# Query projection of an attention layer by Strassen pairs, its gate in two passes, and whole tiles stored at a time

## The chip, the cores and the metric

The kernel runs on one core of a Trainium2 chip. The metric is the device time of one execution in microseconds (us). Engines are named as in the profile: PE is TensorE's matmul, PEld its weight load, DVE VectorE, ACT ScalarE, POOL GpSimd, SP the SyncE queue that only issues DMAs.

## The reference

A two-layer decoder trunk on 1024 tokens of width 1024, in float32: a recurrent layer, an FFN, then one set of keys and values, an attention layer with three branches (compressed, selected, window), a second FFN and a norm. The change touches the queries and gates of the attention layer, and how heads are stored:

```
u = h @ w_q
q = (u[..., :N_HEADS * D_QK] * (D_QK ** -0.5)).reshape(B, S, G, HPG, D_QK)
gates = jax.nn.sigmoid(u[..., N_HEADS * D_QK:] + gate_bias).reshape(B, S, G, HPG, N_BRANCH)
q_rope = apply_partial_rope(q)
```

Here h is the normed residual (1024 tokens x 1024), w_q has 16 heads x 96 + 48 columns, and the 16 heads form 4 groups of 4. The plain q meets the compressed keys, q_rope the selected and window keys.

## The kernel before

**Layout and precision.** Activations lie transposed, features on partitions and tokens along the free dimension: 8 blocks of 128 features x 1024 tokens. A float32 product is made of three matmuls on values split in a high and a low part (`split`, L231 to L234: ACT copies the high part, DVE subtracts it): high x high, high x low, low x high (`mm3`). A projection of one tile of 128 outputs over 512 tokens (`proj`) is thus 8 blocks x 3 = 24 matmuls into one PSUM bank, 48 for all tokens. The norm's row scale is applied to the result (`rb1`, a 128x1024 tile that holds the scale of each token), its feature gain to the operand (`xg`).

**Query tiles.** A group's 4 heads x 96 features are packed in three tiles of 128: two with 64 unrotated features of two heads each (j = 0, 1), one with the 32 others of all four heads (j = 2), of which 24 are rotated (`rope`: a shuffle and three DVE operations of 128x1024). Four groups make 12 tiles.

**Stages.** `run` calls `rglru` (with the first FFN), `kv`, `qphase`, then the rest of the attention and `wo` (with the second FFN). `kv` makes values, the key tiles (`heads`, with `store_split` and `store_heads`), the raw compressed keys and values, and the two compression products (`cmp_hidden`, names ph), between which the query's operands are made: eight loads h1l of the residual from `h1d`, each split by `xg` into xh and xl. `qphase` computes the gate (names pg, gt; its weight has 48 columns, `wn=48`), the rest of the compression (`cmp_out`), then the query tiles group by group (`qheads`, names pn, n). A group is written to three DRAM tensors (`qd`: high part, low part, unrotated), by `store_heads` in eight SP DMAs each, per head. The attention (`attention`) is a generator: its first steps load masks, queries and keys and are taken between the groups, and group 3 is handed to it as filler, of which it takes one half-tile every `FE` = 4 turns of its loop. `load_q` fetches the queries of one of the 32 steps (4 groups x 8 blocks of 128 tokens).

**Strassen form.** The two FFNs are computed with seven products in place of eight (names pa, pb, pc, so, L745): the 8 blocks of features and the 1024 tokens are each halved, so the operand has four parts, and from them come B11, T1, T2, T3, B21, T4, B22. Each product is 4 blocks x 3 = 12 matmuls of 512 tokens, and each weight operand is split by `sop` (128x512) a few products ahead. There two tiles of outputs, gate and value, are a pair.

**Order and buffers.** All large tiles come from one pool of 49 buffers of 128x1024 (`slot`), all PSUM tiles from 8 banks (`ps`). A buffer's next writer waits until its last reader is done, a store's landing included. The order on each engine is fixed when the program is built: a planner takes instructions in program order, those under `high_priority` (weight loads and splits) earlier. `wget` returns the next weight, loads `ld` and splits `sp` ahead.

Of the kernel before, what the change touches and what calls it, by code (L numbers as in the profile page):

```python
# [27 lines left out]
QPRE = 5  # L28
# [12 lines left out]
FIL = 5  # L41
QLT = 1
FI0 = 1
FE = 4
XA = 3
# [26 lines left out]
Q_LAST = Q_ORDER  # L72


class Trunk:
# [44 lines left out]
    def weights(self):  # L120
# [18 lines left out]
        for b in range(2):  # L139
            for j in range(3):  # L140
                w.append((f"k{b}_{j}", d["w_k"][b, j], 1024))
# [4 lines left out]
        for j in range(6):  # L146
            w.append((f"w1k{j}", d["w1_k"][j], 1024))
        for j in range(4):
            w.append((f"w1v{j}", d["w1_v"][j], 1024))
        w.append(("gate", d["w_gate"], 384))  # L150
        w.append(("w2", d["w2"], 320, 0))
        for g in range(4):
            for j in (2, 0, 1):
                w.append((f"q{g}_{j}", d["w_q"][g, j], 1024))
# [30 lines left out]
    def pair_load(self, src, n):  # L185
        def f(t):
            self.nc.sync.dma_start(t.rearrange("p (b c) -> p b c", b=2)[:, :, 0:n],
                                   src[:, :, 0:n].rearrange("b p c -> p b c"))
        return f
# [446 lines left out]
    def sop(self, src):  # L636
        t = self.slot("so", F32R)
        self.split(t[:, 0:512], t[:, 512:1024], src)
        return t
# [698 lines left out]
    def heads(self, keys, xs, rb):  # L1338
        nc = self.nc
        n = []  # L1340
        for key in keys:
            w = self.wget(key)
            t = self.slot("n")
            for c0 in (0, 512):
                p = self.ps("pn")
                self.proj(p, w, xs, c0)
                nc.vector.tensor_tensor(t[:, c0:c0 + 512], p, rb[:, c0:c0 + 512], ALU.mult)
            n.append(t)
        return n
# [10 lines left out]
    def store_heads(self, dst, n):  # L1360
        nc = self.nc
        for h in range(4):
            a = (h % 2) * 64
            nc.sync.dma_start(dst[h, 0:64], n[h // 2][a:a + 64, :])
            nc.sync.dma_start(dst[h, 64:96], n[2][32 * h:32 * h + 32, :])

    def store_split(self, dhi, dlo, n):
        his, los = [], []
        for t in n:
            hi, lo = self.slot("nh", F32R), self.slot("nl", F32R)  # L1370
            self.split(hi, lo, t)
            his.append(hi.bitcast(F32))
            los.append(lo.bitcast(F32))
        self.store_heads(dhi, his)
        self.store_heads(dlo, los)
# [19 lines left out]
    def kv(self, kvp):  # L1395
# [6 lines left out]
        self.kd = self.dram("kd", [2, 2, 4, 96, S])  # L1402
# [36 lines left out]
        for b in range(2):  # L1439
            n = self.heads([f"k{b}_{j}" for j in range(3)], xs, rb)  # L1440
            n[2] = self.rope(n[2])
            self.store_split(self.kd[b, 0], self.kd[b, 1], n)
# [41 lines left out]
        hk = self.cmp_hidden("w1k", imk)  # L1484
        del imk
        self.xq = []

        def xq(k0, k1):
            for k in range(k0, k1):
                h = self.slot("h1l")  # L1490
                nc.gpsimd.dma_start(h, self.h1d[k])
                self.xq.append(self.xg(h, 2, k))

        xq(0, XA)
        hv = self.cmp_hidden("w1v", imv)
        xq(XA, KD)
        return hv, hk

    def cmp_out(self, hv, hk):
        nc = self.nc  # L1500
        w2 = self.wget("w2")
# [37 lines left out]
    def cmp_hidden(self, key, im):  # L1539
# [4 lines left out]
        for q in range(len(im)):  # L1544
            w = self.wget(f"{key}{q}")
            for j in range(4):
                for a, b in ((0, 0), (0, 1), (1, 0)):
# [5 lines left out]
                    i += 1  # L1553
        bias = self.small("hb", 2)
# [6 lines left out]

    def qphase(self, hid):
        nc, d = self.nc, self.d
        xs, self.xq = self.xq, None
        rb = self.rb1
        w = self.wget("gate")
        gt = self.slot("gt")
        for c0 in (0, 512):
            p = self.ps("pg")
            self.proj(p[0:48, :], w, xs, c0, wn=48)  # L1570
            nc.vector.tensor_tensor(gt[0:48, c0:c0 + 512], p[0:48, :], rb[0:48, c0:c0 + 512], ALU.mult)
        nc.scalar.activation(gt[0:48, :], gt[0:48, :], AF.Sigmoid, bias=self.cv[0:48, C_GB:C_GB + 1])
        self.cmp_out(*hid)
        self.qd = [self.dram(f"qd{j}", [4, 4, 96, S]) for j in range(3)]
        def qheads(g):
            nonlocal rb
            n = []
            for j in (2, 0, 1):
                w = self.wget(f"q{g}_{j}")
                t = self.slot("n")  # L1580
                for c0 in (0, 512):
                    p = self.ps("pn")
                    self.proj(p, w, xs, c0)
                    nc.vector.scalar_tensor_tensor(t[:, c0:c0 + 512], p, QSCALE, rb[:, c0:c0 + 512],
                                                   op0=ALU.mult, op1=ALU.mult)
                    if j == 1 and c0:
                        if g == 3:
                            xs.clear()
                    else:
                        yield  # L1590
                n.append(t)
                if j == 2:
                    r2 = self.rope(t)
            n = n[1:] + n[:1]
            if g == 3:
                self.cos = self.sin = self.rb1 = None
                rb = t = w = None
# [674 lines left out]
```

## Time and profile before

| | us |
|---|---|
| median of 3 runs | 2631.3 (2630.43 to 2632.89) |
| the profiled execution | 2628.91 |
| its span on the chip | 2627.1 |
| 1234 to 1265: compression products, ph | 31 |
| 1265 to 1376: gate, rest of the compression, query tiles up to the first half of group 3 | 111 |
| 1376 to 1428: the attention begins, the other five halves as filler | 52 |
| 1428 to 1890: the attention without filler | 462 |

The span is divided by the profile's own time, which begins with the first instruction of the program. Busy times of engines overlap, since they run beside each other; what counts in a stretch is which engine has no gap. Matmuls are pipelined: the duration of one is longer than the distance to the next.

### The profile page before, as it was taken

The page shows a single profiled execution, that of the slowest core. Times are in us where ns is not written, and L with a number is a line of the kernel's source. Part 1 is how long each engine was busy: PE and PEld are TensorE (multiplying, and loading weights), DVE is VectorE, ACT ScalarE, POOL GpSimd, SP SyncE. Part 2 cuts the span into 40 slices and gives each one's busy share as a digit, 9 for nine tenths or more (in the row PEclk, how much of TensorE's full clock was granted, in tenths as well). Part 3 has the DMA queues.
Part 4 walks back from the last instruction along what each step waited for, and adds up shares of the span by engine and source line. Part 5 has one row for each costly group of instructions (what it writes and reads, how often), then busy time and mean ns, then how long its engine had stood idle before and what let it go on. Part 6 is the DMA issues. An engine that isn't in the chain of part 4 may idle for free.

```text
span 2627.1 us, 36460 instructions
## 1 busy us (share of the span) xinstructions
PE 2595.6 (99%) x12490; PEld 2165.5 (82%) x12490; DVE 1856.2 (71%) x3683; ACT 1310.4 (50%) x2573; POOL 934.4 (36%) x1101
## 2 busy tenths in 40 slices
PE   8999999999999999999999999999999999999998
PEld 7887888888888888888888888888887888888886
DVE  7686778655555887537447989988879555557976
ACT  4556656432323544414316888888865223324534
POOL 0111242443434330201004766666543343434333
PEclk9999999999999999999999999999999999999999
DMA  4233796666566993544384412221695666558971
GB/s 161 90 125 114 291 230 179 151 152 152 150 145 179 252 243 80 181 124 156 131 245 128 118 62 70 67 68 47 149 253 138 145 158 163 151 134 224 245 185 64
DMA packets 189160, 400.59 MB, mean 152 GB/s; under 512 B 18592, under 2 KB 68128, under 8 KB 188976
## 3 DMA queue, kind: packets, MB, share of 16 engines
q1 hardware_dynamic: 119280, 245.24, 28.6%
q0 software_dynamic: 68320, 151.09, 27.3%
q8 instruction: 99, 1.62, 0.2%
q10 hardware_dynamic: 1376, 1.94, 0.2%
q14 instruction: 85, 0.70, 0.1%
HBM read 308.55 MB, written 83.36 MB: 149 GB/s over the span
## 4 chain that ended last, share of the span: by engine, by line
PE 80%; DVE 5%; DMA 2%; issue 2%; ACT 0%; POOL 0%; SPq 0%; POOLq 0%; DVEq 0%; ACTq 0%
PE pb L745 13%; PE pa L745 8%; PE pc L745 8%; PE pU L1097 8%; PE pn L241 8%; PE psc L241 6%; PE pV L1097 5%; PE pt L1914 4%; PE pU L1283 3%; PE pW L1097 2%; PE po L1945 2%; PE po L1946 2%; PE py L241 2%; PE pV L1283 2%; PE pkc L241 1%
## 5 line engine op out<-in xcount | busy, mean ns | idle before, releaser
L233 ACT ACTIVATE so<-wr 128x512 fp32r<-128x512 f32 (+1 forms) x504 | 296.2, 612 | 188.6 <-DMA wr<-w_dn 79.2
L234 DVE TENSOR_TENSOR so<-wr,so 128x512 fp32r<-128x512 f32 (+1 forms) x504 | 343.3, 710 | 64.6 <-ACT so L233 63.9
L745 PE MATMUL pb<-so,so 128*128 128x512 f32 x1584 | 381.4, 391 | 4.2 <-DVE so L234 1.8
L745 PEld LDWEIGHTS pb<-so,so 128*128 128x128 f32 x1584 | 298.0, 188 | 67.7 <-DVE so L234 2.3
L745 PE MATMUL pc<-so,so 128*128 128x512 f32 x1056 | 256.2, 389 | 0.0
L745 PE MATMUL pa<-so,so 128*128 128x512 f32 x1056 | 250.9, 389 | 0.0
L1097 PE MATMUL pU<-so,so 128*128 128x512 f32 x1056 | 244.2, 389 | 0.0
L192 POOL DMA_DIRECT2D wr<-w_gu x176 | 162.3, 1068 | 224.3 <-DVE so L234 182.6
L745 PEld LDWEIGHTS pa<-so,so 128*128 128x128 f32 x1056 | 198.3, 188 | 41.1
L745 PEld LDWEIGHTS pc<-so,so 128*128 128x128 f32 x1056 | 198.3, 188 | 41.1
L1097 PEld LDWEIGHTS pU<-so,so 128*128 128x128 f32 x1056 | 198.1, 188 | 41.1
L241 PE MATMUL psc<-kl,ql 96*128 96x512 f32 (+2 forms) x960 | 230.2, 365 | 0.8 <-DVE cst L1738 0.5
L773 ACT ACTIVATE ev<-ev 128x512 f32<-128x512 f32 x44 | 27.8, 632 | 328.8 <-POOL ev L772 328.8
L234 DVE TENSOR_TENSOR thl<-pt,thl 128x512 fp32r<-128x512 f32 x264 | 176.7, 683 | 13.4 <-ACT thl L233 12.2
L241 PEld LDWEIGHTS psc<-kl,ql 96*128 96x128 f32 x960 | 163.8, 189 | 22.1 <-issue 1.1
L233 ACT ACTIVATE thl<-pt 128x512 fp32r<-128x512 f32 x264 | 150.1, 594 | 44.2 <-PE pt L1914 38.0
L234 DVE TENSOR_TENSOR wl<-wr,wh 128x1024 fp32r<-128x1024 f32 (+3 forms) x95 | 104.9, 1112 | 66.8 <-ACT wh L233 55.8
L192 POOL DMA_DIRECT2D wr<-w_dn x96 | 91.0, 1192 | 148.3 <-DVE so L234 62.1
L772 POOL TENSOR_TENSOR ev<-ev,rb 128x512 f32<-128x512 f32 x44 | 59.8, 1359 | 220.1 <-DVE ev L771 220.1
L233 ACT ACTIVATE wh<-wr 128x1024 fp32r<-128x1024 f32 (+3 forms) x95 | 89.6, 964 | 66.4 <-DMA wr<-w_q 19.9
L1097 PE MATMUL pV<-so,so 128*128 128x512 f32 x528 | 121.6, 389 | 0.0
L1097 PEld LDWEIGHTS pV<-so,so 128*128 128x128 f32 x528 | 99.1, 188 | 20.6
(390 smaller groups left out, 5929.2 us busy)
## 6 DMA issues: line engine op xcount, KB each, us to landing
wr<-w_gu SPq DMA_DIRECT2D x110, 512.0 KB, 4.8
wr<-w_gu POOLq DMA_DIRECT2D x176, 256.0 KB, 5.1
zd<-ev SPq DMA_DIRECT2D x44, 512.0 KB, 3.2
zr<-zd SPq DMA_DIRECT2D x44, 512.0 KB, 6.8
wr<-w_dn SPq DMA_DIRECT2D x40, 512.0 KB, 8.6
wr<-w_dn POOLq DMA_DIRECT2D x64, 256.0 KB, 7.7
ql<-qd SPq DMA_DIRECT2D x64, 192.0 KB, 3.2
wr<-w_in SPq DMA_DIRECT2D x23, 512.0 KB, 4.0
```

The source lines that it names most:

```text
L192: self.nc.gpsimd.dma_start(dst, src, accum_op=ALU.add)
L233: nc.scalar.activation(hi, src, AF.Copy)
L234: (nc.gpsimd if pool else nc.vector).tensor_tensor(lo, src, hi.bitcast(F32), ALU.subtract)
L241: self.nc.tensor.matmul(ps, a, b, start=j == 0, stop=j == n - 1)
L745: nc.tensor.matmul(p, a, b, start=k + n == 0 and j in (1, 5, 6), stop=k == 3 and n == 2, skip_group_check=j not in (1, 5, 6))
L772: nc.gpsimd.tensor_tensor(t0[:, hi], t0[:, hi], rb[:, hi], ALU.mult)
L773: nc.scalar.activation(t0[:, hi], t0[:, hi], AF.Silu)
L1097: nc.tensor.matmul(ps, a, b, start=k + n == 0 and j in (1, 5, 2), stop=k == G[g] - 1 and n == 2, skip_group_check=j not in (1, 5, 2))
L1283: nc.tensor.matmul(ps, a, b, start=k + q == 0 and new, stop=k == n - 1 and q == 2, skip_group_check=not new)
L1914: nc.tensor.transpose(pt[:, h * P:(h + 1) * P], Pt[n][h][r][:, off:off + P], self.ident)
L1945: nc.tensor.matmul(po[n], v, thl[:, 0:512], start=False, stop=False)
L1946: nc.tensor.matmul(po[n], v, thl[:, 512:1024], start=False, stop=end)
```

## The change

Eight of the twelve query tiles are computed as four pairs of tiles, each by seven products (84 matmuls) in place of 2 x 48; a new class `Operands` makes B11, T1 and T2 beside the compression products (`side`) and the others in `qphase`, and `Pairs` makes the weight operands, with sums of weights on POOL (`add`). The other four tiles are singles: four products of 12 matmuls on the same operands B11, T1, B21 and B22. They are the filler: six of their 16 products run before the attention's loop, the others every second turn. The gate's weight is laid out as 48 columns of high part, 16 of zero and 48 of low part, so that one pass with the high and one with the low part of the operand take the place of three. The query's scale goes into `rb1`. Each finished tile is stored by itself: unrotated on POOL's queue, high part on ACT's, low part on SP's (or POOL's). The DRAM tensors of keys and queries now hold whole tiles, and `load_k` and `load_q` take the heads out of them, with twice as many DMAs. The eight loads h1l are issued ahead of both compression products.

```diff
-QPRE = 5
+QPRE = 2
-FE = 4
+FE = 2
+Q_PAIRS = 4
+QF = 6
+class Operands:
+    def make(self, name, ks=range(4)):
...
+            if name == "B11":
+                t = k_.slot("so", F32R)
+                nc.scalar.activation(t[:, lo], x1[:, lo], AF.Copy, scale=g1)
+                nc.vector.scalar_tensor_tensor(t[:, hi], x1[:, lo], g1, t[:, lo].bitcast(F32),
+                                               op0=ALU.mult, op1=ALU.subtract)
...
+            if name == "T1":
...
+                nc.gpsimd.tensor_tensor(s, x1[:, hi], x1[:, lo], ALU.subtract)
+                nc.scalar.activation(s, s, AF.Copy, scale=g1)
+            elif name == "T2":
...
+                nc.scalar.activation(x2, x2, AF.Copy, scale=g2)
+                nc.gpsimd.tensor_tensor(s, x2[:, hi], self.t1[u][:, c], ALU.subtract)
...
+            elif name == "T3":
+                s = x1[:, hi]
+                nc.vector.scalar_tensor_tensor(s, x1[:, lo], g1, self.t2[u][:, c], op0=ALU.mult, op1=ALU.subtract)
...
+            elif name == "T4":
+                s = x2[:, lo]
+                nc.vector.tensor_tensor(s, s, self.t2[u][:, c], ALU.subtract)
...
+            out.append(k_.sop(s))
+class Pairs:
+    PROD = {1: ("a", "B11"), 6: ("b", "T2"), 5: ("c", "T1"), 2: ("a", "B21"), 7: ("b", "T3"), 4: ("b", "T4"),
+            3: ("c", "B22")}
...
+    def add(self, out, a, b):
+        self.k.nc.gpsimd.tensor_tensor(out, a, b, ALU.add)
+    def touch(self, f):
...
+        self.add(s[:, lo], v[:, lo], v[:, hi])
+        self.add(v[:, lo], v[:, lo], g[:, lo])
+    def pump(self, n):
...
+                self.ops[(f, j)] = k.sop({1: g[:, lo], 2: g[:, hi], 4: v[:, hi], 7: v[:, lo], 5: s[:, lo],
+                                          6: s[:, hi], 3: s[:, lo]}[j], neg=j == 3)
+                if j == 5:
+                    self.add(s[:, hi], s[:, lo], g[:, lo])
+                elif j == 6:
+                    self.add(s[:, lo], s[:, hi], g[:, hi])
+                    self.touch(f + 1)
...
+    def product(self, i):
...
+        for k in range(4):
...
+            for n, (a, b) in enumerate(((wh, xh), (wh, xl), (wl, xh))):
+                self.k.nc.tensor.matmul(p, a, b, start=k + n == 0 and new, stop=k == 3 and n == 2,
+                                        skip_group_check=not new)
...
+    def store_split(self, dhi, dlo, t, pool=False):
+        hi, lo = self.slot("nh", F32R), self.slot("nl", F32R)
+        self.split(hi, lo, t, pool)
+        self.nc.scalar.dma_start(dhi, hi.bitcast(F32))
+        (self.nc.gpsimd if pool else self.nc.sync).dma_start(dlo, lo.bitcast(F32))
...
+        for k in range(KD):
+            x.h[k] = self.slot("h1l")
+            nc.gpsimd.dma_start(x.h[k], self.h1d[k])
+        sd = side()
+        hk = self.cmp_hidden("w1k", imk, sd)
...
+    def gate(self, x, w):
...
+        def mms(bank, name, k0, start):
...
+            for k in range(4):
+                for c in (lo, hi):
+                    nc.tensor.matmul(banks[bank][0:112, :], w3[:, k0 + k, :], x.X[name][k][:, c],
+                                     start=start and k == 0 and c == lo, stop=k == 3 and c == hi,
+                                     skip_group_check=not start)
+        def fold(dst, bank):
+            p = banks[bank]
+            nc.scalar.activation(dst, p[64:112, :], AF.Copy)
+            nc.vector.tensor_tensor(dst, p[0:48, :], dst, ALU.add)
...
+        seq = [(0, 1), (0, 5), (1, 1), (1, 5), (0, 6), (1, 6), (0, 7), (1, 7), (0, 2), (1, 2), (0, 4), (0, 3)]
+        for f in range(2, Q_PAIRS):
+            seq += [(f, 1), (f, 5), (f - 1, 4), (f - 1, 3), (f, 6)]
+            seq += [(f, 2), (f, 7)] if f < Q_PAIRS - 1 else [(f, 7), (f, 4), (f, 2), (f, 3)]
...
+        def scale(t, c):
+            nc.gpsimd.tensor_tensor(t[:, c], t[:, c], self.rb1[:, c], ALU.mult)
...
+            if j == 6:
+                V(t0[:, hi], t2[:, lo], b, ALU.subtract)
+            elif j == 2:
+                V(t0[:, lo], a, self.rb1[:, lo], ALU.mult)
+            elif j == 7:
+                V(t1[:, hi], b, t2[:, lo], ALU.subtract)
+                V(t1[:, hi], t1[:, hi], c, ALU.add)
+                scale(t1, hi)
+            elif j == 4:
+                V(t1[:, lo], b, t2[:, lo], ALU.subtract)
+                scale(t1, lo)
+            elif j == 3:
+                V(t0[:, hi], t0[:, hi], c, ALU.subtract)
+                scale(t0, hi)
...
+        pr.pump(4)
+        make = {0: "T3", 2: "B21", 4: "T4", 6: "B22"}
+        gates = {0: 2, 12: 1, 14: 1, 23: 1}
+        for i in range(npair):
+            pr.pump(i + 4)
+            for _ in range(gates.get(i, 0)):
+                next(ga)
+            pr.product(i)
+            f, j = seq[i]
+            evict(f, j)
+            if i in make:
+                x.make(make[i])
...
+        for _ in range(QF):
+            next(more)
+        next(att)
```

More of the change, by code (lines that the diff above doesn't have):

```diff
@@ L139, in weights @@
         for b in range(2):
-            for j in range(3):
+            for j in (2, 0, 1):
                 w.append((f"k{b}_{j}", d["w_k"][b, j], 1024))
@@ L1483, in kv, with side, cmp_out @@
         del vst
-        hk = self.cmp_hidden("w1k", imk)
-        del imk
[L1486 to L1496, printed above, removed]
+        x = self.qx = Operands(self, 2)
+        def side():
+            for name in ("B11", "T1", "T2"):
+                for k in range(4):
+                    x.make(name, (k,))
+                    yield
+        for k in range(KD):
[3 more added lines that the diff above has]
+        hk = self.cmp_hidden("w1k", imk, sd)
+        del imk
+        self.qgate = self.gate(x, self.wget("gate"))
+        next(self.qgate)
+        nc.scalar.activation(rb, rb, AF.Copy, scale=QSCALE)
+        hv = self.cmp_hidden("w1v", imv, sd)
+        for _ in sd:
+            pass
         return hv, hk
-    def cmp_out(self, hv, hk):
+    def cmp_out(self, w2, hv, hk):
         nc = self.nc
-        w2 = self.wget("w2")
         self.kcT = self.cpool.tile([96, 4, 64], F32, name="kcT")
@@ L1553, in cmp_hidden @@
                     i += 1
+            next(side, None)
         bias = self.small("hb", 2)
@@ L1618, in qphase @@
[L1618 to L1636 removed]
+        lo, hi = slice(0, 512), slice(512, 1024)
@@ new lines, in post, with fill @@
+        def post(u, pool=False):
+            g, j = Q_TILES[u]
+            n = tiles.pop(u)
+            nc.gpsimd.dma_start(self.qd[2][g, j], n)
+            if j == 2:
+                n = self.rope(n)
+                if g == 3:
+                    self.cos = self.sin = None
+                yield
+            self.store_split(self.qd[0][g, j], self.qd[1][g, j], n, pool)
+            yield
+        def fill():
+            for i in range(npair, len(pr.seq)):
+                pr.pump(i + 3)
+                pr.product(i)
+                f, j = pr.seq[i]
+                evict(f, j)
+                if late:
+                    next(late.pop(0))
+                if j == 3:
+                    u = Q_PAIRS + f
+                    one = post(u, i >= npair + 8)
+                    late.extend([one, one] if Q_TILES[u][1] == 2 else [one])
+                yield
+            x.X.clear()
+            self.rb1 = None
+            while late:
+                next(late.pop(0))
+                yield
```

325 lines of the change are left out of this document (207 added, 118 removed).

## The prediction

> **What bounds the kernel now.** I read the page first, then the busy time by stretch around the query projection, then what TensorE waited for there.
>
> ```profile
> span 2627.1 us, 36460 instructions
> PE 2595.6 (99%) x12490; PEld 2165.5 (82%) x12490; DVE 1856.2 (71%) x3683; ACT 1310.4 (50%) x2573; POOL 934.4 (36%) x1101
> PEclk9999999999999999999999999999999999999999
> ```
>
> TensorE (PE) is busy for 2595.6 of 2627.1 us at full granted clock; every other engine has room on average. In the stretches (columns: us, then busy time and instruction count of PE, PEld, DVE, ACT, POOL, the granted clock, DMA share, GB/s):
>
> ```profile
> 1234.00:1265.00 31.00, 31.00 (x252) 30.36 (x251) 18.33 (x28) 13.99 (x21) 4.31 (x8) 1.00 0.85 316
> 1265.00:1288.00 23.00, 23.00 (x111) 15.48 (x110) 8.52 (x10) 11.28 (x13) 0.00 (x0) 1.00 0.00 1
> 1288.00:1376.00 88.00, 88.00 (x397) 72.72 (x395) 44.31 (x51) 15.35 (x16) 0.00 (x0) 1.00 0.79 222
> 1376.00:1422.00 46.00, 46.00 (x236) 39.33 (x235) 29.37 (x113) 22.90 (x78) 16.32 (x23) 1.00 0.52 148
> 1422.00:1500.00 78.00, 75.09 (x461) 64.86 (x461) 73.68 (x276) 63.52 (x176) 56.95 (x70) 1.00 0.46 123
> ```
>
> From the compression products (1234) to the end of the filler (1422) PE has no gap. After that VectorE (DVE) is at 73.68 of 78 us and PE idles 2.9 us. So in the changed place a matmul removed is time removed, as long as DVE, which has half of 1265 to 1376 free, does not take the place of PE.
>
> **What goes.** Each 128x512 matmul of a long run costs its pitch, not its 389 ns of latency:
>
> ```profile
> 1114.81 65.28 PE pn L241 x288
> L241 PE MATMUL pn<-xh,wh 128*128 128x512 f32 x288 | 111.9, 392 | 0.3 <-DVE n L1584 0.3
> L241 PE MATMUL pg<-xl,wh 128*48 128x512 f32 x16 | 6.3, 393 | 0.0
> ```
>
> The first row is of the chain in order of time: 65.28/288 = 0.2267 us each. The row of pn is one of three terms of 288, 864 in all; 6 of the 18 tiles are the k tiles with 288 of them, and 576 = 12 tiles x 2 halves x 24 are the query's. The gate row is one of three terms of 16: 48 matmuls.
>
> After: a pair of tiles takes 7 products x 12 = 84 matmuls in place of 96. Four pairs take 336 in place of 384, four single tiles 4 x 4 x 12 = 192 as before; the gate, with high and low part of its weight side by side in 112 columns, takes 4 groups x 4 blocks x 2 = 32 in place of 48. Removed: 48 + 16 = 64 matmuls, 64 x 0.2267 = **14.5 us**. A 112-column weight is priced as a 128-column one; if it went like the 48-column rows (393 ns beside 392) nothing changes.
>
> **What comes, beside PE.** The prices:
>
> ```profile
> L234 DVE TENSOR_TENSOR so<-wr,so 128x512 fp32r<-128x512 f32 (+1 forms) x504 | 343.3, 710 | 64.6 <-ACT so L233 63.9
> L233 ACT ACTIVATE so<-wr 128x512 fp32r<-128x512 f32 (+1 forms) x504 | 296.2, 612 | 188.6 <-DMA wr<-w_dn 79.2 <-DMA wr<-w_gu 25.9 <-PE pb L745 23.6
> L765 DVE TENSOR_TENSOR ev<-pb,ev 128x512 f32<-128x512 f32 x44 | 30.3, 688 | 99.8 <-PE pb L745 99.8
> L769 DVE TENSOR_TENSOR ev<-ev,ev 128x512 f32<-128x512 f32 x44 | 32.0, 728 | 4.7 <-DVE ev L768 0.5
> L234 DVE TENSOR_TENSOR nl<-n,nh 128x1024 fp32r<-128x1024 f32 x10 | 12.2, 1222 | 4.5 <-ACT nh L233 4.5
> L1354 DVE STREAM_SHUFFLE sh<-n 128x1024 f32<-128x1024 f32 x6 | 8.0, 1335 | 0.0
> L1355 DVE TENSOR_TENSOR t<-n,cos 128x1024 f32<-128x1024 f32 x6 | 7.2, 1205 | 0.0
> L772 POOL TENSOR_TENSOR ev<-ev,rb x44: 1282/1287/1746, 476.3 to 2404.7; 128x512 f32<-128x512 f32 x44
> ```
>
> DVE over the 28 products of the pairs: 28 weight splits x 0.71 = 19.9; 16 splits of T3, B21, T4, B22 x 0.71 = 11.4; making T3 and T4, 8 x 0.73 = 5.8; evictions, six a pair, 24 x 0.69 = 16.6; splits of eight finished tiles x 1.22 = 9.8; three rotations of 1.34 + 3 x 1.21 = 5.0, so 14.9; the gate's folds and small copies about 3.6 (five at eviction price). Sum **82 us**. PE in the same stretch: 336 + 32 matmuls x 0.2267 = **83.4 us**, and some small ones. DVE is therefore nearly full, 98%, where it was half empty. ScalarE (ACT): 44 splits x 0.61, 8 tile splits, a few copies: under 45 us, no bound. POOL: 10 remaining weight additions and 12 scalings x 1.29 = 28 us, with the eight stores it issues.
>
> The nearest precedent is the FFN, which begins with the same order of products and the same operands T3 to B22, and then runs 7 products a unit:
>
> ```profile
> 460.00:470.00 10.00, 10.00 (x45) 8.26 (x44) 10.00 (x18) 8.32 (x15) 0.00 (x0) 1.00 0.00 1
> 2005.00:2015.00 10.00, 10.00 (x46) 8.29 (x45) 10.00 (x18) 7.08 (x13) 1.64 (x2) 1.00 0.28 60
> 540.00:616.30 76.30, 76.30 (x338) 63.18 (x338) 40.75 (x61) 22.82 (x40) 29.78 (x28) 1.00 0.63 153
> PE pb L745 <- DVE so L234: 1.8, 1, 1.8
> PE pb L745 <- ACT so L233: 1.1, 1, 1.1
> ```
>
> At both starts DVE is full for 10 us and PE hardly notices: no wait in the first layer, 1.8 + 1.1 = 2.9 us in the second (the two rows of waits). The running unit (four in 76.3 us) keeps PE full with DVE at 53%. The query pairs are harder: half of their 28 products are start. Ahead of product 11 DVE owes 16 splits and 8 makings of operands (17.2), about 16 weight splits less the 4 made before (8.5), eight evictions (5.5) and 2 us of gate and compression, 33 us, against 11 x 2.72 = 30 us of products, 3.6 of gate and the small matmuls. That is even. The second half has the other 46 us of DVE (82 less 33 and the four early splits) beside 17 products, 46 us, and 3.6 of gate, and what slips there (rotations, splits of finished tiles) may slip into the six single-tile products that come before the attention's own work, 16 us of PE with about 7 of DVE. Weight splits run four products ahead (10.9 us). I take a stall of **2.9 us** for the whole, that of the second layer's start; the ends are 0 (first layer's start) and the rival below.
>
> The rest costs nothing on PE while its cover holds. B11, T1 and T2 are made beside the compression products: 12 splits (8.5 us of DVE, 7 of ACT), 8 more scalings on ACT and 8 subtractions on POOL (10.3 us) in 31 us in which the old operands xh, xl (8 x 1.28 of DVE) go. Their eight loads are moved ahead of all compression products on POOL's queue:
>
> ```profile
> L1491 POOL DMA_DIRECT2D h1l<-h1d x8: 531/531/585, 1237.7 to 1255.2; - x8
> POOL h1l L1491 <- PE ph L1550: 32.7, 5, 20.8
> ```
>
> Before, these issues waited for buffers that the compression products free (20.8 us the longest). If that persists, the subtractions and the first weight sums queue behind them on POOL; with the last issue at 1255 and 5 us of landing, T2 is ready by about 1268 and is wanted after gate and four products, some 15 us past 1265. If the cover went, the start of the products would slip by those 3 us; that is the size of the stall already taken. Stores: a tile now takes three 512 KB issues, on POOL, ACT and SP, where a group took 24 on SP; the loads of a query step take six issues in place of three.
>
> ```profile
> L215 SPq DMA_DIRECT2D wr<-w_q x8: 327/328/372, 1243.2 to 1294.1; - x8
> SPq L1365 <- DVE n L1584: 31.4, 2, 31.1
> ```
>
> 96 more load issues x 0.33 = 31 us of SP's time over the 470 us of attention, against some 110 store issues fewer; and the queue no longer stands for 31 us behind a tile (second row). ACT's store issues are behind ACT's own split, so ACT waits for nothing new; each costs between SP's 0.33 and POOL's 0.53. The filler is 10 products of 2.72 us every second turn in place of five halves of 5.44 every fourth: 27 us either way. I value all this at zero, between -2.9 us (the idle of 1422 to 1500 recovered) and +2.9 (doubled).
>
> **Sum.** The profiled execution took 2628.91 us, 1.8 more than its span; the median is 2631.3, 2.4 more. 2628.91 - 14.5 + 2.9 = 2617.3 for a profiled one, and 2631.3 - 11.6 = **2619.7** for the median.
>
> **Rivals.** *DVE becomes the bound of the pairs (2630).* POOL and DVE hold each other up:
>
> ```profile
> L775 DVE TENSOR_TENSOR ev<-ev,ev x44: 677/680/1787, 485.6 to 2410.8; 128x512 f32<-128x512 f32 x44
> 697.02 1.30 POOL L774 TENSOR_TENSOR ev<-ev,rb 128x512 f32<-128x512 f32 x1 [0.75 <-ACT ev L773]
> 697.49 1.37 DVE L234 TENSOR_TENSOR so<-wr,so 128x512 fp32r<-128x512 f32 x1
> 698.37 1.65 POOL L763 TENSOR_TENSOR ev<-ev,rb 128x512 f32<-128x512 f32 x1
> 698.79 1.78 DVE L775 TENSOR_TENSOR ev<-ev,ev 128x512 f32<-128x512 f32 x1
> ```
>
> A DVE instruction of 0.68 us that begins inside a POOL one takes 1.37 and 1.78: it loses 0.7 to 1.1. The 22 POOL operations would take 15 to 24 us from DVE if all met such an instruction; DVE then needs 97 to 106 us against 83.4, and 13.6 us of stall give 2631.3 - 14.5 + 13.6 = 2630.4 (at the upper end 2639). For it: two thirds of DVE's 82 us (the splits, the making and most of the rotations) read two buffers. Against it: in the FFN unit three such POOL operations cost DVE little (710 on average against about 680), and late tile work may slip. The Trainium skill says so as a rule (SBUF — State Buffer, "Who interferes with whom"): a VectorE instruction with two SBUF inputs contends with a GpSimd one that reads SBUF, and the loser blocks for the whole instruction. The trace agrees: 1.37 and 1.78 us beside 0.68. By that rule alone the time would be this rival's.
>
> *Slower: operands wait for stores (2653).* All tiles share one pool of 49 buffers; 28 operand buffers for the pairs leave about 18. A weight split whose buffer was a store's must wait for its landing:
>
> ```profile
> ACT wh L233 <- DMA qd<-n: 15.7, 1, 15.7
> DVE wl L234 <- DMA qd<-nl: 8.2, 1, 8.2
> qd<-nh SPq DMA_DIRECT2D x16, 256.0 KB, 3.7
> ```
>
> That wait exists already, though PE did not feel it. If it used up the lead of four products, a product would take 3.7 + 0.61 + 0.71 = 5.0 us in place of 2.72. Stores exist from product 12 on: 16 x 2.3 = 37 us, less 14.5, gives 2631.3 + 22 = 2653. It decides from 9 products on (9 x 2.3 = 20.7 us, the gain and 0.2%). Against it: stores are fewer and on three queues.
>
> *No stall at all (2616.8, or 2613.9 with the 2.9 us after 1422 recovered).* For it: the first layer's start. Against it: 98% DVE.
>
> **Chances.** Forecast with its stall of 1 to 7 us 0.53; no stall 0.15; DVE bound 0.23; slower by buffers 0.09. A measurement of this kernel tells 0.2% (5.3 us) from no change: faster means below 2626.0. Of the DVE rival, a quarter ends still below that; so faster 0.53 + 0.15 + 0.06 = 0.74, same 0.17, slower 0.09. The range goes from 2613.9 to 2631 and leaves out the buffers and the far end of the DVE rival.
>
> **What would show it.** Right: 64 matmuls fewer, PE busy lower by about 14 us, waits of PE on splits of T3 to B22 of 1 to 7 us in the first twelve products, DVE over 90% there. Wrong: PE waiting on weight splits through all pairs with long DVE instructions under POOL ones (DVE bound); ACT or DVE splits released by stores with PE behind them (buffers); or more than 5 us idle after the filler ends, when the late tile work lands on the attention's full DVE.

## The result and the profile after

| | before | after |
|---|---|---|
| median of 4 runs each, same chip, us | 2631.78 (2630.43 to 2632.89) | 2655.38 (2654.2 to 2656.26) |
| ratio, 95% interval | 1 | 1.009 (1.0072 to 1.0107) |
| span of the profiled execution, us | 2627.1 | 2654.5 |
| first score product, us | 1382.7 | 1397.5 |
| last score product, us | 1874.6 | 1898.3 |

The changed kernel is 23.6 us slower; 2619.7 was forecast. The head of the page of the profile after:

```profile
span 2654.5 us, 36544 instructions
PE 2599.2 (98%) x12426; PEld 2164.0 (82%) x12426; DVE 1908.6 (72%) x3746; ACT 1342.1 (51%) x2638; POOL 1003.7 (38%) x1155
```

The 64 matmuls are gone (12490 - 12426), but PE is busy for 3.6 us *more* than before, not 14.5 less. Had the others kept their pace, PE would show 2595.6 - 14.5 = 2581.1: so 18.1 us of its busy time are matmuls that ran slower. Its idle time rose from 2627.1 - 2595.6 = 31.5 to 2654.5 - 2599.2 = 55.3, by 23.8. The span's change is then -14.5 + 18.1 + 23.8 = +27.4 us. The clock row of the page, in slices of 66 us and tenths, shows nothing of the slower matmuls; short stretches of the profile after do (stretch, its length, then busy time and count of PE, PEld, DVE, ACT, POOL; granted clock, DMA share, GB/s):

```profile
1270.20:1276.90 6.70, 5.49 (x12) 3.90 (x13) 5.63 (x10) 2.10 (x4) 2.72 (x2) 0.50 0.00 0
1410.00:1416.90 6.90, 6.69 (x20) 5.66 (x21) 5.00 (x12) 2.01 (x6) 5.25 (x5) 0.51 0.41 134
2010.80:2021.00 10.20, 10.20 (x33) 8.68 (x32) 5.61 (x11) 4.96 (x10) 3.23 (x3) 0.50 0.49 79
```

With three more, from 1338.3 to 1345.2, 1365.6 to 1369.0 and 1502.2 to 1505.6, there are six such stretches at half clock. PE is busy for 34.1 us in them, of which half, 17 us, is loss: 7 ahead of the first score product, 5 in the attention, 5 behind it. The profile before has one such stretch, of 3.4 us (1.7 lost), so this is some 15 of the 18.1 us.

Where it happened follows from the table: up to the first score product 14.8 us were lost where 14.5 should have been won, so 29.3 us went there; the attention between first and last score product grew by 8.9 us, and the rest of the program by 3.7 (29.3 + 8.9 + 3.7 = 41.9 = 27.4 + 14.5). The stretches that the prediction used, with the same columns, in the profile after:

```profile
1234.00:1265.00 31.00, 31.00 (x251) 30.55 (x250) 26.59 (x33) 24.77 (x38) 18.32 (x15) 1.00 0.86 329
1265.00:1288.00 23.00, 18.40 (x80) 13.81 (x78) 20.02 (x24) 12.48 (x24) 15.54 (x10) 0.85 0.14 46
1288.00:1376.00 88.00, 75.50 (x306) 58.07 (x307) 69.38 (x82) 29.21 (x43) 27.53 (x22) 0.94 0.37 143
```

The compression stage is as full as before, so the operands made beside it cost PE nothing there. In the pairs PE does 80 matmuls where it did 111, and 306 where it did 397, and the granted clock falls to 0.85 and 0.94. DVE is *not* full: 69.38 of 88 us. What PE waited for from 1230 to 1500 (columns: engine, tile, line, releaser; us in total, times, longest):

```profile
PE pa L198 <- ACT so L371: 10.7, 3, 7.3
PE pa L198 <- DVE so L372: 4.4, 3, 1.7
PE pc L1952 <- DMA qr<-qd: 2.0, 1, 2.0
```

All long waits are for weight operands (so): their high part comes from ACT, their low part from DVE. The longest, 7.3 us, read in the timeline of the profile after (columns: start, duration, engine, line, operation, count; in brackets the idle time before it and what ended it):

```profile
1326.88 1.21 DVE L1495 TENSOR_TENSOR sh<-sh,sin 128x1024 f32<-128x1024 f32 x1
...
1329.93 2.71 POOL L1734 TENSOR_TENSOR gt<-gt,rb 48x1024 f32<-48x1024 f32 x1 [0.70 <-DVE gt L1733]
1330.31 0.67 DVE L1795 TENSOR_TENSOR n<-pb,qe 128x512 f32<-128x512 f32 x1
1330.91 5.26 DVE L1496 TENSOR_TENSOR sh<-sh,t 128x1024 f32<-128x1024 f32 x1
1332.61 1.26 POOL L146 TENSOR_TENSOR wr<-wr,wr 128x512 f32<-128x512 f32 x1
1333.84 1.25 POOL L146 TENSOR_TENSOR ws<-ws,wr 128x512 f32<-128x512 f32 x1
1335.06 3.46 POOL L1763 TENSOR_TENSOR n<-n,rb 128x512 f32<-128x512 f32 x2
1336.20 1.06 ACT L371 ACTIVATE nh<-sh 128x1024 fp32r<-128x1024 f32 x1 [11.68 <-DVE sh L1496]
1337.28 1.28 ACT L1735 ACT_TABLE_LOAD   x1
1338.57 1.15 ACT L1735 ACTIVATE gt<-gt,cv 48x1024 f32<-48x1024 f32 x1
1339.63 1.14 ACT L371 ACTIVATE so<-wr 128x512 fp32r<-128x512 f32 x2
1340.30 5.72 PE L198 MATMUL pa<-so,so 128*128 128x512 f32 x14 [7.28 <-ACT so L371]
```

Read it from the top. The last step of a rotation (sh, L1496) is of the size of its sister at 1326.88 that took 1.21 us, but begins inside a POOL instruction, and POOL follows with two more without a gap. The third of them ends at 1335.1 and DVE's instruction at 1336.2, 1.1 us later: it took 5.26 us, as if it had run only when the three were done. The DVE instruction ahead of it (n, L1795) lies inside the same POOL instruction and takes its usual 0.67 us; one of its two inputs (pb) is in PSUM, while L1496 reads both from SBUF. ACT's next instruction in its fixed order is the split of this rotated tile (nh), so ACT stands idle for 11.68 us, although raw weights of a coming pair (wr) are there by 1332.6, when POOL reads them. After it come the gate's table load and sigmoid, and only then the weight split (so, 1339.63) for which PE has stood 7.28 us. When PE resumes, 14 matmuls take 5.72 us, 0.41 each in place of 0.2267: PE's loss goes on after the wait. The Trainium skill has both halves of this as rules. By "SBUF — State Buffer", "Who interferes with whom", a VectorE instruction with two SBUF inputs and a GpSimd one that reads SBUF exclude each other for a whole instruction; the trace agrees, but one VectorE instruction here waited through three. By "TensorE: Matmul & The Clock Gate", "Part 1: The HAM clock gate (the "warmup" mystery)", TensorE drops to half clock after an idle window of about 3.4 us and returns after a busy one; 0.41 beside 0.2267 us behind a gap of 7.28 us agrees (granted clock 0.51 from 1338.3 to 1345.2).

The start of the pairs shows the same hold in its milder form, VectorE and POOL taking turns, in the timeline of the profile after:

```profile
1264.15 1.62 POOL L146 TENSOR_TENSOR wr<-wr,wr 128x512 f32<-128x512 f32 x1
1265.73 1.74 POOL L146 TENSOR_TENSOR ws<-ws,wr 128x512 f32<-128x512 f32 x1
1266.32 1.71 DVE L372 TENSOR_TENSOR so<-tu,so 128x512 fp32r<-128x512 f32 x1
1266.43 0.47 ACT L1693 ACTIVATE hid<-ph,hb 128x252 f32<-128x252 f32 x1 [4.03 <-DVE hb L1692]
...
1269.62 0.68 DVE L372 TENSOR_TENSOR so<-tu,so 128x512 fp32r<-128x512 f32 x1
...
1270.21 1.22 PE L198 MATMUL pa<-so,so 128*128 128x512 f32 x2 [2.69 <-ACT so L371]
1271.22 1.05 PE L198 MATMUL pc<-so,so 128*128 128x512 f32 x2
...
1273.49 4.58 PE L198 MATMUL pa<-so,so 128*128 128x512 f32 x12 [1.21 <-DVE so L372]
```

While POOL adds weights (L146), a split takes DVE 1.7 us; as soon as POOL stops, the same split takes 0.68. ACT stands 4.03 us for a small copy of DVE (hb) that is behind the held ones in DVE's order, with the first weight splits behind it in its own. PE then waits 2.69 us, does four matmuls, waits 1.21 us more, and its next twelve take 4.58 us, 0.38 each; the clock is at half from the first of the four on (0.50 from 1270.2, above). And the lead of four products that the prediction counted on does not exist, as four rows of the same timeline show:

```profile
1299.43 0.63 ACT L371 ACTIVATE so<-wr 128x512 fp32r<-128x512 f32 x1 [2.09 <-PE pb L198]
1300.11 3.30 PE L198 MATMUL pa<-so,so 128*128 128x512 f32 x12 [0.72 <-ACT so L371]
1303.44 0.63 ACT L371 ACTIVATE so<-wr 128x512 fp32r<-128x512 f32 x1 [3.38 <-PE pa L198]
1305.96 2.88 PE L198 MATMUL pa<-so,so 128*128 128x512 f32 x12
```

ACT's split is released by a product of PE that has just ended (pb, then pa): its output buffer is one that this product gives back. The split was asked for four products before, but all buffers are taken. For the first split PE has stood 0.72 us when it is made; the second is ready at 1304.1, 1.9 us before its product begins at 1305.96, less than one product of 2.72. So a delay of ACT or DVE of 2 us reaches PE here. And ACT is delayed, as its own waits from 1265 to 1380 in the profile after show (columns as above):

```profile
ACT nh L371 <- POOL n L1763: 19.6, 3, 12.4
ACT nh L371 <- DVE sh L1496: 18.1, 2, 11.7
```

For 37.7 of these 115 us ACT stands at the split of a finished tile (nh) whose scaling on POOL or rotation on DVE is late, with the weight splits behind it in its order. Not each such wait costs PE something: behind the one of 11.7 us PE stands 7.28, while beside the longest, which ends at 1377.9, PE has no gap.

### The profile page after: what moved, and what is told of

It is laid out like the page before. It is cut to its first block, busy times and chain, and to the rows that moved or that the text cites. A ratio compares the mean times of both kernels' runs of the same rounds, so it can differ in the third digit from the quotient of the medians.

```text
span 2654.5 us, 36544 instructions
## 1 busy us (share of the span) xinstructions
PE 2599.2 (98%) x12426; PEld 2164.0 (82%) x12426; DVE 1908.6 (72%) x3746; ACT 1342.1 (51%) x2638; POOL 1003.7 (38%) x1155
## 4 chain that ended last, share of the span: by engine, by line
PE 76%; DVE 6%; issue 3%; DMA 2%; ACT 1%; POOL 1%; SPq 0%; POOLq 0%; ACTq 0%; DVEq 0%
PE pb L888 13%; PE pa L888 9%; PE pc L888 8%; PE pU L1240 8%; PE psc L379 6%; PE pV L1240 4%; PE pt L2149 4%; PE pU L1426 3%; PE pn L379 2%; PE po L2181 2%; PE po L2180 2%; PE pW L1240 2%; PE py L379 2%; DVE so L372 2%; PE pV L1426 2%
## 5 line engine op out<-in xcount | busy, mean ns | idle before, releaser
L371 ACT ACTIVATE so<-wr 128x512 fp32r<-128x512 f32 (+1 forms) x528 | 310.9, 612 | 202.4 <-DMA wr<-w_dn 89.2
L372 DVE TENSOR_TENSOR so<-wr,so 128x512 fp32r<-128x512 f32 (+1 forms) x528 | 361.8, 714 | 69.5 <-ACT so L371 68.9
L372 DVE TENSOR_TENSOR wl<-wr,wh 128x1024 fp32r<-128x1024 f32 (+2 forms) x82 | 91.3, 1119 | 45.2 <-ACT wh L371 43.3
L2181 PE MATMUL po<-thl,vl 128*128 128x512 f32 x264 | 110.1, 417 | 0.0
```

The lines of the kernel that those rows point to most:

```text
L371: nc.scalar.activation(hi, src, AF.Copy)
L372: (nc.gpsimd if pool else nc.vector).tensor_tensor(lo, src, hi.bitcast(F32), ALU.subtract)
L2181: nc.tensor.matmul(po[n], v, thl[:, 512:1024], start=False, stop=end)
```

## The experiments

Theory A: POOL instructions that read SBUF hold DVE, and DVE holds ACT and PE. Theory B: DVE has too much work of its own in the pairs, whoever runs beside it. A third theory, of the queue: rotations and tile splits stand ahead of weight splits in ACT's and DVE's order. A fourth, theory C of the expectations: too few buffers. Kernels whose text says that they leave something out compute something else than the reference. Differences are against the kernel before on the same chip; the changed kernel's is +23.6 us.

**Weight sums on DVE.** The sharpest test of A against B: 16 additions move from POOL to DVE, which has more work by it.

```diff
     def add(self, out, a, b):
-        self.k.nc.gpsimd.tensor_tensor(out, a, b, ALU.add)
+        self.k.nc.vector.tensor_tensor(out, a, b, ALU.add)
```

> The weight sums of the pairs (16 additions of 128x512) are done by VectorE in place of GpSimd. Theory A (GpSimd's two-input operations hold VectorE up: 0.68 us operations last 1.7 us beside them): VectorE loses about 0.7 to 1.1 us per GpSimd addition and pays 0.69 for its own, so the time falls, to 2640 to 2650 us against 2655. Theory B (VectorE has simply too much work of its own, 82 us beside 83 us of TensorE): 11 us more work on it, time 2660 to 2668. Theory C (weight splits wait for buffers of stores): unchanged, 2652 to 2658.

Measured 2644.41 (4 runs), ratio 1.0048 (1.0031 to 1.0064), +12.7 us. DVE does 16 x 0.7 = 11 us more and the kernel is 11 us faster than the change. B falls. In the windows of this kernel:

```profile
1265.00:1300.00 35.00, 32.92 (x150) 25.12 (x149) 30.31 (x50) 16.15 (x29) 1.12 (x1) 1.00 0.09 31
1300.00:1340.00 40.00, 32.19 (x123) 24.32 (x123) 37.44 (x43) 15.28 (x21) 16.01 (x11) 0.87 0.35 131
```

and in those of the changed one:

```profile
1265.00:1300.00 35.00, 28.91 (x123) 21.74 (x121) 28.68 (x38) 16.30 (x30) 15.54 (x10) 0.90 0.09 30
1300.00:1340.00 40.00, 30.90 (x128) 23.37 (x128) 34.03 (x34) 13.96 (x21) 19.62 (x15) 0.98 0.25 96
```

Up to 1300, where POOL has only sums, DVE does 50 instructions in 30.31 us in place of 38 in 28.68 and PE 150 matmuls in place of 123. From 1300 to 1340, where POOL's scalings and gate product remain, PE is as starved as before, but not by the same hold, as the timeline of this kernel shows:

```profile
1320.67 5.13 POOL L1734 TENSOR_TENSOR gt<-gt,rb 48x1024 f32<-48x1024 f32 x1 [5.17 <-issue]
1322.18 1.21 DVE L1496 TENSOR_TENSOR sh<-sh,t 128x1024 f32<-128x1024 f32 x1
1325.83 1.15 ACT L1735 ACTIVATE gt<-gt,cv 48x1024 f32<-48x1024 f32 x1 [7.96 <-POOL gt L1734]
```

Here the last rotation step takes its usual 1.21 us and POOL is the one held: its gate product lasts 5.13 us in place of 2.71. ACT stands 7.96 us for that result, which the sigmoid needs, and PE 4.96 us for the weight split behind it. So POOL starves PE in two ways, by holding DVE and by being late itself with a result that stands in ACT's order.

**Sums that only write.** The sums are left out; `add` fills its output with a constant: same buffers and order, POOL reads nothing in it, and its operations are shorter.

```diff
-        self.k.nc.gpsimd.tensor_tensor(out, a, b, ALU.add)
+        self.k.nc.gpsimd.memset(out, 0.5)
```

> The weight sums are left out: GpSimd fills the same buffers with a constant, so it writes and reads nothing; everything else stands. Theory A: VectorE's splits beside these fills last 0.68 us again, time 2630 to 2645. Theory B: VectorE's work is the same, 2650 to 2658. Theory C: the same, 2650 to 2658.

Measured 2641.0 (one run), +9.3. The gain of 14 us without any change of buffers or of DVE's work agrees with A. POOL's writes are also shorter than its sums were, so this run does not tell reading from time, and no other does.

**No sums at all,** which frees two buffers a pair as well:

```diff
-        s = k.slot("ws")
-        self.add(s[:, lo], v[:, lo], v[:, hi])
-        self.add(v[:, lo], v[:, lo], g[:, lo])
+        s = g
...
-                    self.add(s[:, hi], s[:, lo], g[:, lo])
+                    pass
...
-                    self.add(s[:, lo], s[:, hi], g[:, hi])
```

> The weight sums are left out: the products take raw weights, so GpSimd makes no additions and the pairs hold two buffers fewer. Theory A: 2620 to 2640. Theory B: 2650 to 2658. Theory C: 2645 to 2655, since fewer buffers are held.

Measured 2640.51 (one run), +8.8, half a us outside theory A's range and within 0.5 us of the run above: the two buffers show no worth here beside the sums. The second stall stands, with the gate product as the holder, in this kernel's timeline:

```profile
1318.44 2.39 POOL L1731 TENSOR_TENSOR gt<-gt,rb 48x1024 f32<-48x1024 f32 x1 [6.87 <-DVE gt L1730]
1318.77 3.13 DVE L1493 TENSOR_TENSOR sh<-sh,t 128x1024 f32<-128x1024 f32 x1
1322.00 1.06 ACT L368 ACTIVATE nh<-sh 128x1024 fp32r<-128x1024 f32 x1 [8.34 <-DVE sh L1493]
1326.10 2.26 PE L195 MATMUL pa<-so,so 128*128 128x512 f32 x4 [4.82 <-ACT so L368]
```

**Nothing on POOL that reads tiles in the pairs:** the run above without the scalings and the gate product either.

```diff
-        nc.gpsimd.tensor_tensor(gt[0:48, :], gt[0:48, :], self.rb1[0:48, :], ALU.mult)
...
         def scale(t, c):
-            nc.gpsimd.tensor_tensor(t[:, c], t[:, c], self.rb1[:, c], ALU.mult)
+            pass
```

> On top of the run without weight sums, GpSimd's scalings of the finished tiles and its product for the gate are left out too, so GpSimd computes nothing while the pairs run. Theory A: the stall of 4.8 us behind the rotation goes too, 2624 to 2633. Theory C: the lead of the splits is as short as before, 2636 to 2641.

Measured 2622.72 beside 2628.95 of the kernel before (one run each), -6.2, just below theory A's range and below all 31 runs of the kernel before on record (lowest 2628.27). With DVE's and ACT's splits, rotations and order as they are in the change, the loss turns into a gain, so POOL's work beside the pairs is what the loss hangs on. The run takes away both of its ways at once, the hold on DVE and the late results in ACT's order; it does not tell their shares. A window of this kernel and, behind it, the busy times of its page:

```profile
1300.00:1340.00 40.00, 38.72 (x175) 31.38 (x174) 34.59 (x48) 19.41 (x28) 2.71 (x5) 1.00 0.48 188
```

```profile
PE 2583.5 (99%) x12426; PEld 2154.9 (82%) x12426; DVE 1890.1 (72%) x3746; ACT 1341.0 (51%) x2638; POOL 950.7 (36%) x1122
```

PE does 175 matmuls in place of 128 at full clock, and its busy time over the span is 2583.5, 2.4 from the 2581.1 that 64 matmuls less should give. DVE has 48 instructions in 34.59 us, 0.72 each, in place of 34 in 34.03. By the spans (2620.8 beside 2627.1) 8.2 of the 14.5 us are still lost: 4.3 before the first score product, 1.8 in the attention, 2.1 after it. ACT's waits at finished tiles are not gone (14.6 us behind rotations and 12.8 behind another DVE step from 1265 to 1380, none over 8.7), yet PE waits for operands (so) only 2.6 us from 1230 to 1500. That fits a loss by the long waits with a weight split due behind them.

**The queue.** The three rotations left out, POOL as in the change:

```diff
             if j == 2:
-                n = self.rope(n)
```

> The changed kernel without the rotation of the query tiles (its four VectorE operations of 1.2 to 1.3 us for each third tile are left out); GpSimd's work stands. If the queue behind the rotation is a main cause (ACT's split of a rotated tile waits for VectorE's last rotation step, held 5.3 us by GpSimd, and the next weight split stands behind it on ACT): the stall of 7.3 us at 1333 us goes with the slow clock after it, time 2636 to 2646. If GpSimd's reads alone decide (theory A without the queue): VectorE loses a little less, 2648 to 2654. If full buffers decide (theory C, now in the form that a split waits for the buffer that the product before it frees): 2648 to 2655.

Measured 2644.45 beside 2628.95 (one run each), +15.5, in the range of the queue as a main cause. The window of this kernel:

```profile
1300.00:1340.00 40.00, 40.00 (x183) 32.74 (x181) 33.67 (x39) 19.13 (x28) 22.95 (x17) 1.00 0.49 184
```

POOL is busier than ever (22.95 us) and PE is full: without the rotation in front, a held DVE does not empty PE here. In these runs, then, the second stall needs both, the POOL instructions and the order. The first stall, at 1265 to 1300, needs no rotation: PE did 29.92 us of 35 there in this run too.

**Lead and buffers.** With the sums left out, weight splits asked for six products ahead in place of four; and, on the change itself, the queries of five attention steps in place of two loaded ahead.

```diff
-        pr.pump(4)
+        pr.pump(6)
...
-            pr.pump(i + 4)
+            pr.pump(i + 6)
```

> The run without weight sums, with weight splits asked for six products ahead in place of four. If all 49 buffers are taken (theory C), asking earlier changes nothing or costs: 2638 to 2650 against 2640.5. If the lead of four is what lacks: 2630 to 2637.

```diff
-QPRE = 2
+QPRE = 5
```

> The changed kernel with the first five query blocks loaded before the attention's loop, as before the change, in place of two. The attention stage takes 8.9 us longer than before from its first to its last score product. If late query loads begin that (TensorE waits 2.0 us for one at 1410 us): 2650 to 2653. If it is the filler's form or the clock: 2654 to 2657. If buffers are short: more than 2657.

Measured 2639.18, +10.2 (beside +8.8 with four), and 2665.42, +36.5 (beside +23.6), one run each: a longer lead gives nothing, and taking buffers costs 13 us (one weight split on ACT stands 8.8 us behind a query load, so <- DMA qr<-qd). Both fit a pool of buffers that is full in this stage. A larger pool was not tried.

**Sums by DMA.** The sums built in their buffers by loads that accumulate:

```diff
-        self.add(s[:, lo], v[:, lo], v[:, hi])
-        self.add(v[:, lo], v[:, lo], g[:, lo])
+        k.nc.sync.dma_start(s[:, lo], d["w_qb"][f, :, hi])
+        k.acc(s[:, lo], d["w_qb"][f, :, lo])
+        k.acc(v[:, lo], d["w_qa"][f, :, lo])
```

> The weight sums are made by accumulating DMAs from DRAM, as in the FFNs; GpSimd issues 16 DMAs (about 1 us each) in place of 16 additions, and each pair loads 256 KB more. Theory A: VectorE is held up only by the 12 scalings, the gate's product and the subtractions for T1 and T2; time 2622 to 2640. Theory B: VectorE's work is the same, 2650 to 2658. Theory C: the same or worse, 2650 to 2662.

Measured 2649.17 (4 runs), ratio 1.0071 (1.0056 to 1.0086), +17.5: theory A's range is missed. A window of this kernel:

```profile
1265.00:1300.00 35.00, 28.80 (x128) 22.00 (x126) 21.14 (x36) 16.04 (x30) 7.11 (x9) 0.95 0.60 119
```

DVE is relieved (36 instructions in 21.14 us, 0.59 each) and PE still does only 128 matmuls: sums that go by DMA come late (ACT stands 13.2 us for them between 1255 and 1300, so <- DMA ws<-w_qb), and PE waits for the splits of them. POOL's reads are not the only way to starve these products.

**Without scalings on POOL, computing the reference.** The token scale is multiplied into the operand ahead of the stage (loaded, multiplied by rb on DVE beside the key tiles, stored), so scalings and gate product go; the weight sums stay on POOL in the first kernel and go to DVE in the second.

```diff
             for j in (2, 0, 1):
+                for k in ((0, 1), (2,), (3,), (4, 5), (6,), (7,))[3 * b + (2, 0, 1).index(j)]:
+                    t = self.slot("hx")
+                    nc.gpsimd.dma_start(t, self.h1d[k])
+                    nc.vector.tensor_tensor(t, t, rb, ALU.mult)
+                    nc.gpsimd.dma_start(self.h1s[k], t)
...
-        nc.gpsimd.tensor_tensor(gt[0:48, :], gt[0:48, :], self.rb1[0:48, :], ALU.mult)
...
-                scale(t1, hi)
```

> The token scale is multiplied into the operand beside the key tiles (eight VectorE products of 1.22 us in a stretch where VectorE is half free, stored and loaded again) in place of into each finished tile; the scalings and the gate's product on GpSimd go, the low halves are evicted by ScalarE. The weight sums stay on GpSimd. Theory A: the stall behind the rotation goes, the stalls of the first ten products stay: 2630 to 2642. If only all GpSimd work together, or only the sums, matter: 2648 to 2656.

> As the run before, with the weight sums on VectorE: no GpSimd computing beside the pairs, but 16 x 0.69 = 11 us of VectorE. Theory A: 2622 to 2634, near the run in which GpSimd computes nothing (2622.7), plus what the 11 us cost on a full VectorE. If VectorE's own load is the limit: 2634 to 2645.

The first: 2633.25 (10 runs) beside 2630.07 (19 runs), ratio 1.001 (1.0001 to 1.002), +3.2: 20 us better than the change with the sums still on POOL. (The edit also lets ACT evict the tiles' low halves and frees the buffer of rb1 earlier, so not all of the 20 us need be the scalings'.) The second: 2625.7 (10 runs, 2623.92 to 2631.03), ratio 0.9981 (0.9972 to 0.9991), -4.4 us: its interval lies below the kernel before, though by less than the 5.3 us that the prediction took as the least that counts. Windows of the first, then of the second (whose profile is that of its slowest execution, 2631.03):

```profile
1265.00:1300.00 35.00, 29.42 (x127) 22.34 (x126) 29.76 (x41) 16.89 (x31) 15.39 (x10) 0.90 0.09 30
1300.00:1340.00 40.00, 38.33 (x171) 30.42 (x169) 33.13 (x42) 19.88 (x30) 11.68 (x9) 1.00 0.41 158
```

```profile
1265.00:1300.00 35.00, 33.88 (x157) 26.43 (x156) 32.40 (x56) 18.95 (x35) 0.00 (x0) 1.00 0.09 31
1300.00:1340.00 40.00, 39.56 (x176) 31.44 (x176) 36.23 (x50) 19.89 (x30) 2.18 (x4) 1.00 0.48 184
```

Each place of the stall goes with its own work on POOL. Up to 1300 PE does 123 matmuls in the change and 127 without scalings, but 150 and 157 with the sums on DVE; from 1300 to 1340 it does 128 and, with the sums on DVE, 123, but 171 and 176 without scalings and gate product. In the second kernel DVE is at 32.4 of 35 and 36.2 of 40 us, 92%, and PE keeps its pace: the fullness of DVE was not the trouble.

**Sums made in DRAM.** To have neither engine add, the sums were made in DRAM by accumulating DMAs that the program's text places beside the value tiles (44 more issues on POOL's queue) and loaded like weights, once with the scaled operand and once on the change.

```diff
+        self.wqv, self.wqs = self.dram("wqv", [Q_PAIRS, P, S]), self.dram("wqs", [Q_PAIRS, P, S])
...
-        s = k.slot("ws")
-        self.add(s[:, lo], v[:, lo], v[:, hi])
-        self.add(v[:, lo], v[:, lo], g[:, lo])
+        g, v, s = [k.wget(f"{self.key}{c}{f}") for c in "gvt"]
```

> As e9, with the weight sums made earlier by accumulating DMAs from DRAM to DRAM beside the value tiles and loaded like weights: neither GpSimd nor VectorE computes them. Theory A: 2616 to 2626, under the kernel before and the run in which GpSimd computes nothing (2622.7, whose operands and evictions still cost VectorE more). If the extra DMAs (44 issues on GpSimd's queue, about 12 MB written) disturb the value and key tiles: 2626 to 2640.

> The changed kernel with the weight sums made in DRAM, the scalings left on GpSimd. Theory A: as without sums, 2636 to 2644.

Measured 2641.6 (4 runs), ratio 1.0043 (1.0028 to 1.0058), +11.5; and 2653.73 (one run), +23.7. Both miss theory A's range, and the first lies just past its second range too. The loss is not where that second range looked for it. The sums depend on nothing but the program's inputs, and the 44 issues went out from 2.0 to 77 us on POOL's queue, at the very start of the program. The first 70 us of the first of these kernels:

```profile
0.00:70.00 70.00, 51.67 (x194) 39.16 (x195) 40.81 (x71) 28.28 (x31) 30.66 (x46) 0.95 1.03 298
```

PE is busy for 51.67 us where the kernel with scaled operand and sums on DVE has 62.33, at a DMA share of 1.03 beside 0.42. The first matmul of the tiles py comes at 63.3 in place of 48.5, the compression products begin at 1251.1 in place of 1235.3, and the attention at 1388.9 in place of 1373.8. Nearly all of the lag is there by 63 us; from the compression products to the first score product this kernel takes 137.8 us and the other 138.5. What the same issues would cost if they were held back to a later stage was not tried.

## Why the prediction was wrong

**The 14.5 us of matmuls: right.** 64 are gone, and without readers on POOL PE's busy time falls by 2595.6 - 2583.5 = 12.1 us.

**Operands beside the compression, loads moved ahead, the gate in one width: right in the main.** PE is full from 1234 to 1265, the gate's first 16 matmuls take 0.24 us each, and no wait of PE is for the loads. One part was late: the low parts of T2 (four so<-tu on DVE) were made from 1266.3 to 1272.8, ahead of the first weight splits in DVE's order.

**DVE's 82 us beside 83.4 of PE: the sum was about right and the inference from it wrong.** DVE shows 20.02 + 69.38 = 89 us busy from 1265 to 1376, with the time in which it was held; without POOL's reads it is 81 us from 1265 to the first score product, single products included. In the scaled version with sums on DVE it is 92% busy and PE hardly waits. The trouble was not a sum of work but single instructions that last 1.7 to 5.3 us in place of 0.7 to 1.2.

**The failed step: "I take a stall of 2.9 us", from the second FFN's start.** The stage lost 29.3 us, ten times as much. The FFN was the nearest precedent by the order of products, not by what POOL does beside it: POOL was idle in the first layer's start and had 1.64 us in the second's, both rows quoted then. The two waits of the second start lie at 1983 and 1985.5, and there POOL only issued DMAs. Here it had 15.5 us in the first 23. The price was also short of the precedent's own, since a slow stretch follows those waits in the profile before:

```profile
1985.70:1989.10 3.40, 3.40 (x9) 2.65 (x9) 3.40 (x7) 3.40 (x8) 2.59 (x3) 0.50 0.54 90
```

What stood in its place: PE was busy for 28.91 of the 35 us up to 1300 and for 30.90 of the 40 up to 1340, because POOL's sums, scalings and gate product held DVE, and ACT's weight splits stood behind what DVE and POOL had not finished.

**The rival "DVE becomes the bound" had the mechanism and was given 0.23.** Its size was off by four omissions. It charged 0.7 to 1.1 us to each pair of instructions; the run shows a DVE instruction held through three POOL ones, and the gate product of 2.71 us among them. It let DVE's loss reach PE only where DVE ran out of time (13.6 us); in fact ACT, which has a split in its order behind the held instruction, stopped too. And it had no slow matmuls, some 7 us of them ahead of the first score product. It also left out that POOL is held too and is late with what ACT needs (5.13 us for a gate product of 2.71, in the run with the sums on DVE). The prediction's reason against it, that "late tile work may slip", fell with the run without rotations: the order is fixed, and the rotation stood *ahead* of the weight splits.

**"Weight splits run four products ahead (10.9 us)": wrong.** Asking is not having: with all buffers taken one split came 0.7 us too late and the next 1.9 us ahead (the rows from 1299 to 1306), and asking six ahead gave nothing.

**The rival of buffers held by stores (2653) is near in number only.** Splits did wait for buffers, nearly always for such as a product of PE frees. From 1265 to 1380 one weight split on ACT stood behind a store (so <- DMA qd<-nl), for 1.4 us.

**The filler and stores at zero, between -2.9 and +2.9: outside.** The attention grew by 8.9 us. Its rows, before from 1382.7 and after from 1397.5, first to last score product:

```profile
1382.70:1874.60 491.90, 488.00 (x2986) 427.39 (x2985) 434.53 (x1619) 402.36 (x1106) 304.02 (x398) 1.00 0.28 82
```

```profile
1397.50:1898.30 500.80, 493.14 (x2987) 430.58 (x2986) 436.37 (x1624) 406.55 (x1112) 309.85 (x405) 0.99 0.27 81
```

The same matmuls take 5.1 us more and PE idles 3.8 us more. The 5.1 are the two stretches at half clock at 1410 and 1502, which follow waits of PE of 1.98 us (for a query load) and 1.96 us. In the run without POOL's reads the attention costs 493.7 and has no such stretch, though PE waits 2.2 us for query loads there; so the slow clock can't be put down to POOL's reads by these runs, and what carries the 3.8 us of idle time stays open. Of the 3.7 us after the last score product, 3.4 are the clock: at the start of the second FFN PE waits 1.11 and 1.82 us in both profiles, and 3.4 us at half clock follow in the one before, 10.2 us in the one after. The waits are the same in both, so these profiles show no price of the change there.

## What to carry to other kernels

Before work is put on GpSimd as "the free engine", look at what VectorE does in that stretch: if it is dense with two-buffer instructions on which the bound engine depends, 16 additions cost less on a VectorE that is 92% busy than on an idle GpSimd beside it. A sum of busy times does not show whether a producer keeps up: check that the lead of the operands really exists (who releases the buffer that each is written to), and what stands ahead of the next operand in the fixed order of all engines that make it. And price a gap of TensorE at more than its length: here 18.1 us of slower matmuls came on top of 23.8 us of idle time, some of them behind gaps that the kernel before has too. Work that depends only on the program's inputs may be issued long before the place where its line stands: look in the timeline where it went.

## What the runs showed of the hardware

A VectorE instruction that begins inside a GpSimd one can be held through several that follow without a gap: 5.26 us in place of 1.21, behind instructions of 2.71, 1.26 and 1.25 us. Where the two alternate, a split of 0.68 us takes 1.7 and a 128x512 addition on GpSimd 1.6 to 1.7.

Either engine can be the one held: with the sums on DVE, POOL's gate product took 5.13 us in place of 2.71 and the rotation step beside it its usual 1.21. A VectorE instruction with one of its inputs in PSUM, begun inside the gate product of 2.71 us, took its usual 0.67 us.

The granted clock fell to half for 3.4 to 10.2 us not only after a gap of PE of 7.28 us (0.41 us each matmul) but also after gaps of 2.69 us (0.38 each), 1.98, 1.96 and 1.50 us, none of these four as long as the window that the Trainium skill gives ("TensorE: Matmul & The Clock Gate", "Part 1: The HAM clock gate (the "warmup" mystery)"). After one of 1.68 us, which ended at 1385.6, it did not fall, and the same two gaps of 1.11 and 1.82 us were followed by 3.4 us at half clock in one profile and 10.2 in another; what decides it, no run here tells.
